# A list schedule with new planner costs: queue time apart from an instruction's end, port waits between VectorE and GpSimd, transfers by row length and with later operands

## The chip, the cores and the metric

The kernel runs on one core of one Trainium2 chip. A core has five engines that run side by side, each through a queue of its own in a fixed order: TensorE (PE, matrix products and transposes), ScalarE (ACT), VectorE (DVE), GpSimd (POOL) and SyncE (SP), which here issues all DMA transfers. An engine waits on semaphores for another engine's or a transfer's result. The metric is the time of the program on the device in microseconds (us), the median of several runs; lower is better.

## What is computed

One inference step of an encoder of two layers, for a prompt of 2048 frames and for 8 running streams of 16 new frames each, in 32-bit floating point:

```python
def prompt_layer(x, g, w_in, w_out, rel_bias, conv_w, subln_g, lam, lam_init):
    B, S, _ = x.shape
    h = rmsnorm(x, g)
    a_q, a_k, a_v, a_g, b_b, b_c, b_h, b_g, c_q, c_k, c_v, c_g = split_projection(h, w_in)
...
    o_a = band_attention_prompt(a_q.reshape(B, S, A_HEADS, HEAD_DIM), k, v, rel_bias)
...
    up = jnp.pad(b_c * b_h, ((0, 0), (CONV_WIDTH - 1, 0), (0, 0)))
    o_b = b_b * causal_conv(up, conv_w, S)
...
    o = diff_attention_prompt(cq, ck, cv, lam)
    o_c = (rmsnorm(o, subln_g, SUBLN_EPS) * (1.0 - lam_init)).reshape(B, S, C_WIDTH)
    y = x + merge_branches(o_a, a_g, o_b, b_g, o_c, c_g, w_out)
    return y, (k[:, S - keep:], v[:, S - keep:], up[:, -(CONV_WIDTH - 1):], ck, cv)
```

Branch A (8 heads) attends to the own chunk of 64 frames and 8 chunks before it, with a learned bias; B is a gated convolution of width 3; C (4 heads) takes softmax(Q1K1) - lam softmax(Q2K2) over the whole past. Each is multiplied by silu of its gate, and `w_out` brings the three back to 1024 columns.

The sample layer does the same for the running streams, over their cached keys and values. A last norm follows the second layer. Keys, values and the convolution's last rows are outputs too.

## The kernel before

The prompt is cut into 4 segments of 512 frames; a round is one segment of one layer, so there are 8 rounds. In each round a branch is a row of steps: projections (`proj_t`, `proj_n`), attention of a head (`a_attn` for A, `c_attn` for C), the convolution (`b_half`), gates, the output projection of the round before (`out_proj`) and the norm of the next one (`norm`). The small steps of the running streams (`a_sample`, `c_sample`) are put in between as tasks. Each operand of a projection is split into a high and a low part (`ah`, `al`; `whi`, `wlo`), and three matmuls take the place of one. A weight tile of 128x512 is loaded by SP (`w`, two buffers), and POOL makes `whi` and `wlo` of it (five buffers each). In an attention the scores go to PSUM (tile `s`), DVE adds the bias and takes the row's minimum (`arow` in A, `row` in C, the minimum in `sm`), ACT takes the exponential, TensorE transposes the row (tile `t`), ACT and DVE split the result into `pth` and `ptl`, and TensorE multiplies both with the values (tile `o`). In branch C q and k come back from DRAM (`cz`) through two transfers each of 64 rows of 4 KB (`q_stack`, `k_stack`). A norm takes a power of -0.5 on POOL (`rms_rows`); so does the norm of a head's output (`c_post`).

The program is not issued in the order in which it is written. Every operation is first recorded (`Program.add`), with the engine, a planned cost (`duration`), its predecessors and the buffers that it uses. `order` then plays the engines through time: of the five, that engine goes on which can start earliest, and it takes, of its instructions whose operands and buffers are there at that time by the plan, the one that was written first (projections count as written 350 places later, `LATER`). `issue` sends the instructions in that order. So the planned times have one effect, the order in each engine's queue; on the chip each queue runs in that order, and waits where the plan was wrong. `ORDER` (a list of steps for each segment) sets the order in which they are written, and is the same before and after.

Before, an instruction's end by the plan is its start plus its cost, and a user on another engine can start `LATENCY[engine][user's engine]` ns later. A transfer costs its queue 55 ns; its end is worked out from a descriptor time of 470 ns each, a start of 935 ns, 360 bytes a ns over one bus, and 850 ns.

Of the kernel before, what the change touches and what calls it, by code (L numbers as in the profile page):

```python
# [11 lines left out]
F32R = mybir.dt.float32r  # L12
BF16 = mybir.dt.bfloat16
AF = mybir.ActivationFunctionType
ALU = mybir.AluOpType
# [84 lines left out]
class Ins:  # L100
    __slots__ = ("eng", "op", "a", "k", "cost", "need", "ready", "succ", "end", "bufs", "dma", "prio", "index")


class Program:
# [5 lines left out]
    LATENCY = ((0, 198, 196, 200, 200), (270, 153, 141, 120, 140), (256, 128, 127, 155, 125), (203, 170, 65, 96, 70), (200, 110, 145, 130, 130))  # L110
# [35 lines left out]
    def duration(self, eng, op, outs, reads, k):  # L146
# [5 lines left out]
        psum = any(v.tile.tag.psum for v in big + [o for o in outs if isinstance(o, View)])  # L152
        if eng == self.PE:
            rhs = k.get("rhs")
            return 2.5 + (max(107, n / 2.4) if isinstance(rhs, View) and rhs.dt == F32R else n / 1.2)
        if eng == self.ACT:
            return (51 if psum else 93) + n / 1.2 + (186 if "accum_out" in k else 0)
        if eng == self.DVE:
            if op == "tensor_reduce":
                n = math.prod(m for _, m in big[0].v.ap[1:])  # L160
            slow = psum or len(big) > 1 or op == "tensor_reduce"
            return 70 + n / (0.96 if slow else 1.92) + (60 if len(views) > len(big) or "accum_out" in k else 0)
        return 52 + n * (2.3 if len(big) > 1 else 1.05)

    def add(self, name, op, a, k):
# [6 lines left out]
        if op == "dma_start":  # L172
            o = outs[0].v if isinstance(outs[0], View) else outs[0]
            i.cost = 55.0
            i.dma = 4.0 * math.prod(m for _, m in o.ap)
        else:
            i.cost = self.duration(i.eng, op, outs, reads, k)
        i.need, i.ready, i.succ, i.end = 0, 0.0, [], None
        i.index = len(self.ins)
# [32 lines left out]
    def order(self):  # L212
# [5 lines left out]
        dge = bus = active = 0.0  # L218
# [6 lines left out]
        def give(tag):  # L225
            while tag.head < len(tag.queue) and tag.free:
# [5 lines left out]
                for j in u.users:  # L232
                    j.need -= 1
                    j.ready = max(j.ready, t + self.LATENCY[e][j.eng])
# [11 lines left out]
        for _ in range(len(self.ins)):  # L246
# [24 lines left out]
            free[e] = t + cost  # L271
            i.end = t + cost
            if i.dma is not None:
                dge = max(dge, t + 50) + 470
                bus = max(bus, dge + 935) + i.dma / 360
                i.end = bus + 850
            out.append((t, i))
            for j in i.succ:
                j.need -= 1
                lat = self.LATENCY[e if i.dma is None else 4][j.eng]  # L280
                j.ready = max(j.ready, i.end + lat)
                if j.need == 0:
                    ready(j)
            for b in i.bufs:
                b.left -= 1
                b.end = max(b.end, (i.end, e if i.dma is None else 4))
# [1101 lines left out]
```

## Time and profile before

| | |
|---|---|
| time, median of 3 runs | 3269.55 us (3258.78 to 3273.34) |
| the profiled execution's own time | 3262.4 us |
| its span, first to last instruction | 3260.7 us |
| mean granted clock of TensorE | 0.991 |
| TensorE busy | 3055.7 us (94%), 20416 instructions |
| VectorE busy | 2326.3 us (71%) |
| ScalarE busy | 1782.0 us (55%) |
| GpSimd busy | 1648.2 us (51%) |
| share of 16 DMA engines, queue of SP | 57.1% |

The profile is of one execution. A row of instructions names the line that issues them, the engine, the operation, what is written and read by the program's names (`o<-ptl,cv`: PSUM tile `o` from `ptl` and `cv`), shape and count. All recorded operations have line 305, since `issue` sends them all; so groups are read by their tiles. A matmul's end is modelled, and matmuls overlap, so that the sum of their durations is more than the time.

### The profile page before, as it was taken

The page shows a single profiled execution, that of the slowest core. Times are in us where ns is not written, and L with a number is a line of the kernel's source. Part 1 is how long each engine was busy: PE and PEld are TensorE (multiplying, and loading weights), DVE is VectorE, ACT ScalarE, POOL GpSimd, SP SyncE. Part 2 cuts the span into 40 slices and gives each one's busy share as a digit, 9 for nine tenths or more (in the row PEclk, how much of TensorE's full clock was granted, in tenths as well). Part 3 has the DMA queues.
Part 4 walks back from the last instruction along what each step waited for, and adds up shares of the span by engine and source line. Part 5 has one row for each costly group of instructions (what it writes and reads, how often), then busy time and mean ns, then how long its engine had stood idle before and what let it go on. Part 6 is the DMA issues. An engine that isn't in the chain of part 4 may idle for free. (4 is left out here: it accounts for less than half of the span.)

```text
span 3260.7 us, 60379 instructions
## 1 busy us (share of the span) xinstructions
PE 3055.7 (94%) x20416; PEld 2764.5 (85%) x20416; DVE 2326.3 (71%) x5753; ACT 1782.0 (55%) x3817; POOL 1648.2 (51%) x1789
## 2 busy tenths in 40 slices
PE   7999899899999999999999999999899999999998
PEld 7888888788898888987888888888688988889878
DVE  3667778678685866878556576777867858587884
ACT  2654456465473654657445454665555646565652
POOL 5344564445636375453745446444555355744454
PEclk9999999999999999999999999999999999999999
DMA  6665565565655455554575655746666465655543
GB/s 209 206 183 162 162 207 169 178 191 174 199 154 167 139 186 159 161 151 128 189 220 182 179 159 182 212 150 193 213 205 189 139 185 186 190 151 159 175 119 101
DMA packets 438278, 567.51 MB, mean 174 GB/s; under 512 B 88016, under 2 KB 245200, under 8 KB 437968
## 3 DMA queue, kind: packets, MB, share of 16 engines
q1 hardware_dynamic: 437968, 563.65, 57.1%
q8 instruction: 161, 2.64, 0.3%
q14 instruction: 149, 1.22, 0.1%
HBM read 443.67 MB, written 119.84 MB: 173 GB/s over the span
## 5 line engine op out<-in xcount | busy, mean ns | idle before, releaser
L305 POOL TENSOR_SCALAR whi<-w 128x512 fp32r<-128x512 f32 x640 | 455.6, 712 | 1159.3 <-PE mm L305 705.1
L305 POOL TENSOR_TENSOR wlo<-w,whi 128x512 fp32r<-128x512 f32 x640 | 873.3, 1365 | 57.2 <-PE mm L305 8.4
L305 PE MATMUL mm<-whi,ah 128*128 128x256 f32 x2560 | 734.9, 288 | 8.3 <-ACT ah L305 5.9
L305 PE MATMUL mm<-wlo,ah 128*128 128x256 f32 x2560 | 738.0, 289 | 0.3 <-POOL wlo L305 0.2
L305 PE MATMUL mm<-whi,al 128*128 128x256 f32 x2560 | 737.2, 288 | 0.0
L305 PE MATMUL mm<-ah,whi 128*128 128x512 f32 (+2 forms) x1600 | 591.0, 370 | 7.0 <-DVE mi L305 2.3
L305 PE MATMUL mm<-al,whi 128*128 128x512 f32 (+2 forms) x1600 | 587.1, 367 | 0.0
L305 PE MATMUL mm<-ah,wlo 128*128 128x512 f32 (+2 forms) x1600 | 587.0, 368 | 0.0
L305 ACT ACTIVATE arow<-arow,sm 128x640 f32<-128x640 f32 (+4 forms) x560 | 421.1, 768 | 158.0 <-DVE sm L305 154.9
L305 PEld LDWEIGHTS mm<-whi,ah 128*128 128x128 f32 x2560 | 492.2, 193 | 15.4 <-ACT ah L305 6.2
L305 DVE TENSOR_TENSOR ptl<-t,pth 128x512 fp32r<-128x512 f32 (+3 forms) x800 | 400.7, 520 | 137.0 <-ACT pth L305 85.2
L305 PEld LDWEIGHTS mm<-wlo,ah 128*128 128x128 f32 x2560 | 492.9, 193 | 5.6 <-POOL wlo L305 0.7
L305 ACT CAST pth<-t 128x512 fp32r<-128x512 f32 (+3 forms) x800 | 346.3, 453 | 276.3 <-PE t L305 97.3
L305 PEld LDWEIGHTS mm<-whi,al 128*128 128x128 f32 x2560 | 492.9, 193 | 4.5
L305 ACT ACTIVATE row<-row,sm 128x512 f32<-128x512 f32 (+15 forms) x256 | 308.5, 1206 | 192.8 <-DVE sm L305 191.7
L305 PEld LDWEIGHTS mm<-ah,whi 128*128 128x128 f32 x1600 | 303.0, 190 | 39.6 <-POOL whi L305 2.9
L305 PEld LDWEIGHTS mm<-ah,wlo 128*128 128x128 f32 x1600 | 303.2, 190 | 28.8
L305 PEld LDWEIGHTS mm<-al,whi 128*128 128x128 f32 x1600 | 303.8, 190 | 27.9
L305 PE MATMUL t<-ident,arow 128*128 128x128 f32 x1280 | 240.7, 278 | 11.2 <-ACT arow L305 4.8
L305 PE MATMUL t<-ident,row 128*128 128x128 f32 x1360 | 214.3, 279 | 34.6 <-DVE row L305 31.3
L305 DVE SCALAR_TENSOR_TENSOR row<-row,sm,row 128x1024 f32<-128x1024 f32 (+6 forms) x115 | 199.3, 1733 | 50.8 <-POOL sm L305 44.6
L305 PE MATMUL s<-kst,qq 128*128 128x320 f32 (+4 forms) x896 | 219.8, 328 | 16.1 <-DVE sm L305 7.5
(162 smaller groups left out, 5716.6 us busy)
## 6 DMA issues: line engine op xcount, KB each, us to landing
w<-in_w_in SPq DMA_DIRECT2D x512, 256.0 KB, 3.2
w<-in_w_out SPq DMA_DIRECT2D x128, 256.0 KB, 3.1
v2a<-avh SPq DMA_DIRECT2D x112, 256.0 KB, 3.6
ch<-cz SPq DMA_DIRECT2D x96, 256.0 KB, 4.5
bias<-nbias SPq DMA_DIRECT2D x64, 320.0 KB, 3.8
avh<-qq SPq DMA_DIRECT2D x32, 512.0 KB, 3.6
q<-cz SPq DMA_DIRECT2D x64, 256.0 KB, 4.7
k<-cz SPq DMA_DIRECT2D x64, 256.0 KB, 5.9
```

Source lines behind the costliest of these rows:

```text
L305: getattr(engines[i.eng], i.op)(*[real(x) for x in i.a], **{n: real(x) for n, x in i.k.items()})
```

## The change

It edits the planner alone, in five places.

- `LATENCY` is replaced by smaller numbers, and `TAIL` is new: an engine is free for its next instruction after the cost, but the instruction ends `TAIL` later (170, 98, 83, 30 ns on PE, ACT, DVE, POOL), and users wait from that end.
- `duration` has new figures: a matmul of fp32r operands 14 + n/2.37 ns, at least 113; the power on POOL 370 + 163n; a DVE instruction with an accumulator no longer 60 ns more; others by some ns.
- Port waits: `i.port` marks DVE instructions with no PSUM operand (some kinds apart). One that starts while a POOL instruction runs by the plan is lengthened by what is left of that less 200 ns; a POOL instruction that starts while such a DVE instruction runs, by what is left less 100 ns.
- `transfer` times a DMA by the length of its contiguous runs, with 1.7 times as much for 64 partitions of long runs; its queue is busy 400 ns for each, and no more than 8 are under way.
- `LATE`: an instruction of SP counts as ready 500 ns later than its operands and buffers are.

```diff
-    LATENCY = ((0, 198, 196, 200, 200), (270, 153, 141, 120, 140), (256, 128, 127, 155, 125), (203, 170, 65, 96, 70), (200, 110, 145, 130, 130))
+    LATENCY = ((0, 36, 37, 87, 100), (53, 12, 32, 78, 60), (54, 34, 14, 83, 60), (54, 34, 34, 83, 60), (123, 23, 88, 150, 60))
+    TAIL = (170, 98, 83, 30)
+    LATE = 500
...
-            return 2.5 + (max(107, n / 2.4) if isinstance(rhs, View) and rhs.dt == F32R else n / 1.2)
+            return max(113, 14 + n / 2.37) if isinstance(rhs, View) and rhs.dt == F32R else 4 + n / 1.2
         if eng == self.ACT:
-            return (51 if psum else 93) + n / 1.2 + (186 if "accum_out" in k else 0)
+            return (51 if psum else 93) + n / 1.2 + (94 if "accum_out" in k else 0) + (94 if small else 0)
         if eng == self.DVE:
+            if op == "memset":
+                return 20 + n / 1.25
...
-            return 70 + n / (0.96 if slow else 1.92) + (60 if len(views) > len(big) or "accum_out" in k else 0)
-        return 52 + n * (2.3 if len(big) > 1 else 1.05)
+            return 70 + n / (0.96 if slow else 1.92) + (62 if small or n == 1 and len(big) > 2 else 0)
+        if op == "tensor_tensor" and k["op"] == ALU.pow:
+            return 370 + 163 * n
+        if op == "tensor_tensor":
+            return 70 + n * 2.32
+        return (80 if op == "memset" else 200 if n < 64 else 90) + n * (0.8 if op == "memset" else 1.0)
+
+    @staticmethod
+    def transfer(out, src):
+
+        runs, total = [], 4.0
+        for x in (out, src):
+            ap = x.v.ap[1:] if isinstance(x, View) else x.ap
+            run = 4
+            for st, m in reversed([d for d in ap if d[1] > 1]):
+                if 4 * st != run:
+                    break
+                run *= m
+            runs.append(min(run, 4096))
+        for _, m in (out.v if isinstance(out, View) else out).ap:
+            total *= m
+        if isinstance(out, View) and out.v.ap[0][1] == 64 and min(runs) > 2048:
+            total *= 1.7
+        return total * max(1.1 / 380, (8.5 + min(runs) / 28) / (16 * min(runs)))
...
-            i.cost = 55.0
-            i.dma = 4.0 * math.prod(m for _, m in o.ap)
+            i.cost = 400.0
+            i.dma = self.transfer(outs[0], reads[0])
...
+        i.port = i.eng == self.DVE and op not in ("memset", "reciprocal", "tensor_reduce") and not any(
+            isinstance(x, View) and x.tile.tag.psum for x in reads + outs)
...
+        gp, dv = (0.0, 0.0), (0.0, 0.0)
+        landed = []
+        late = lambda j: self.LATE if j.eng == self.SP else 0
...
-                    j.ready = max(j.ready, t + self.LATENCY[e][j.eng])
+                    j.ready = max(j.ready, t + self.LATENCY[e][j.eng] + late(j))
...
-            free[e] = t + cost
-            i.end = t + cost
             if i.dma is not None:
-                dge = max(dge, t + 50) + 470
-                bus = max(bus, dge + 935) + i.dma / 360
-                i.end = bus + 850
+                if len(landed) >= 8:
+                    t = max(t, landed[-8] + 60)
+                free[e] = t + cost
+                bus = max(bus, t + cost + 1200) + i.dma
+                i.end = max(bus + 900, t + cost + 900)
+                landed.append(i.end)
+            elif e == 0:
+                free[e] = t + cost
+                i.end = free[e] + self.TAIL[0]
+            else:
+                i.end = t + cost + self.TAIL[e]
+                if i.port and gp[0] <= t < gp[1]:
+                    i.end += max(0, gp[1] - t - 200)
+                if e == self.POOL and dv[0] <= t < dv[1]:
+                    i.end += max(0, dv[1] - t - 100)
+                free[e] = i.end - self.TAIL[e]
+                if e == self.POOL:
+                    gp = t, i.end
+                if i.port:
+                    dv = t, i.end
```

What it moves is seen at three places in the queues. In the rows, a tile's name carries the number of its buffer; the line is 305 before and 352 after.

**Place 1**, TensorE, first round: the first score matmuls of branch C (`s<-k,q`), which need q and k from DRAM; `mm` are projections. Before:

```order
L305 MATMUL mm_129<-wlo_107,ah_96 128x256
L305 MATMUL mm_129<-whi_102,al_97 128x256
L305 MATMUL mm_129<-whi_103,ah_96 128x256
L305 MATMUL s_131<-k_111,q_110 128x128
L305 MATMUL s_132<-k_111,q_110 128x128
L305 MATMUL mm_129<-wlo_108,ah_96 128x256
```

After:

```order
L352 MATMUL mm_129<-whi_104,ah_96 128x256
L352 MATMUL mm_129<-wlo_109,ah_96 128x256
L352 MATMUL mm_129<-whi_104,al_97 128x256
L352 MATMUL mm_130<-whi_102,ah_96 128x256
L352 MATMUL mm_130<-wlo_107,ah_96 128x256
L352 MATMUL s_131<-k_111,q_110 128x128
L352 MATMUL s_132<-k_111,q_110 128x128
L352 MATMUL mm_130<-whi_102,al_97 128x256
```

The same score matmul stands at place 393 of TensorE's queue before and at place 418 after, 25 later; the projections of `whi_103` and of two more weight tiles now go ahead of it.

**Place 2**, DVE and TensorE, last segment of the first layer: the splits `ptl<-t,pth` of a head of branch C and the add `mi<-mm,mi` of the output projection, which needs a part of x from DRAM. DVE before:

```order
L305 TENSOR_TENSOR ptl_127<-t_135,pth_125 128x512
L305 TENSOR_TENSOR ptl_128<-t_133,pth_126 128x512
L305 RECIPROCAL sm_85<-sm_94 128x1
L305 TENSOR_TENSOR mi_74<-mm_130,mi_74 128x512
L305 RECIPROCAL sm_92<-sm_91 128x1
L305 TENSOR_TENSOR ptl_127<-t_134,pth_125 128x512
L305 TENSOR_TENSOR ptl_128<-t_135,pth_126 128x512
```

DVE after:

```order
L352 TENSOR_TENSOR ptl_127<-t_134,pth_125 128x512
L352 TENSOR_TENSOR ptl_128<-t_135,pth_126 128x512
L352 ISA arow_68,sm_86<-s_132,bias_70,sm_86 128x320
L352 ISA sm_86 128x1
L352 TENSOR_TENSOR ptl_127<-t_133,pth_125 128x512
L352 RECIPROCAL sm_95<-sm_93 128x1
L352 TENSOR_TENSOR ptl_128<-t_134,pth_126 128x512
L352 TENSOR_TENSOR ptl_127<-t_135,pth_125 128x512
```

The same add now stands 13 instructions behind the split that it stood in front of, and a row minimum of branch A (`arow`) is between the splits. On TensorE, the two products of that split before:

```order
L305 MATMUL o_136<-pth_125,cv_117 128x256
L305 MATMUL mm_129<-whi_101,al_97 128x256
L305 MATMUL mm_129<-whi_101,ah_96 128x256
L305 MATMUL mm_129<-wlo_106,ah_96 128x256
L305 MATMUL mm_129<-whi_101,al_97 128x256
L305 MATMUL mm_129<-whi_102,ah_96 128x256
L305 MATMUL mm_129<-wlo_107,ah_96 128x256
L305 MATMUL o_136<-ptl_127,cv_117 128x256
```

And after:

```order
L352 MATMUL o_136<-pth_125,cv_117 128x256
L352 MATMUL t_135<-ident_138,row_63 128x128
L352 MATMUL t_135<-ident_138,row_64 128x128
L352 MATMUL t_135<-ident_138,row_63 128x128
L352 MATMUL s_132<-kst_120,qq_121 128x320 x2
L352 MATMUL o_136<-ptl_127,cv_117 128x256
```

Three transposes and two score matmuls of branch A stand between the two products, in place of six projections.

**Place 3**, TensorE, second segment of the second layer, a task of the running streams (`a_sample`): transposes of its row, whose splits go to `v2a`, and the products with the cached values (`o<-ch,v2a`). Before:

```order
L305 MATMUL t_133<-ident_138,arow_65 128x128 x4
L305 MATMUL t_135<-ident_138,arow_65 128x128
L305 MATMUL mm_130<-ah_98,wlo_107 128x512
L305 MATMUL mm_130<-ah_98,whi_102 128x512
L305 MATMUL mm_130<-al_99,whi_102 128x512
L305 MATMUL mm_130<-ah_98,wlo_107 128x512
L305 MATMUL mm_130<-ah_98,whi_102 128x512
L305 MATMUL mm_130<-al_99,whi_102 128x512
L305 MATMUL mm_130<-ah_98,wlo_107 128x512
L305 MATMUL o_136<-ch_113,v2a_123 128x256 x4
```

After:

```order
L352 MATMUL s_131<-ptl_128,qq_121 128x512
L352 MATMUL s_131<-pth_125,qq_121 128x512
L352 MATMUL s_132<-kst_120 128x128 x3
L352 MATMUL t_133<-ident_138,arow_65 128x128 x4
L352 MATMUL t_135<-ident_138,arow_65 128x128
L352 MATMUL s_131<-pth_126,qq_122 128x512
L352 MATMUL s_131<-ptl_127,qq_122 128x512
L352 MATMUL s_131<-pth_126,qq_122 128x512
L352 MATMUL o_136<-ch_113,v2a_123 128x256 x4
```

Three score matmuls of another task stand between, in place of seven projections, and other score matmuls of the tasks (`s<-kst`), which stood behind these products, now stand ahead of the transposes.

## Rows read from the trace of the kernel before

**Rows 1.** The page's head and its first part: busy time of each engine, share of the span, number of instructions.

```profile
span 3260.7 us, 60379 instructions
PE 3055.7 (94%) x20416; PEld 2764.5 (85%) x20416; DVE 2326.3 (71%) x5753; ACT 1782.0 (55%) x3817; POOL 1648.2 (51%) x1789
```

**Rows 2.** TensorE's waits over the whole span: its instruction's output tile, who ended the wait, then us in total, number of waits, and the longest.

```profile
PE t L305 <- DVE row L305: 31.3, 35, 9.8
PE s L305 <- DVE sm L305: 20.6, 33, 1.8
PE o L305 <- DVE ptl L305: 18.3, 26, 2.5
PE t L305 <- DVE mi L305: 11.9, 12, 3.6
PE o L305 <- DVE v2a L305: 10.7, 8, 4.6
PE s L305 <- DMA k<-cz: 8.4, 8, 1.9
PE s L305 <- POOL wlo L305: 8.0, 6, 2.2
PE s L305 <- POOL qq L305: 7.2, 8, 2.5
PE s L305 <- DVE ptl L305: 6.0, 13, 1.2
...
PE t L305 <- ACT arow L305: 4.8, 9, 1.4
PE s L305 <- DVE row L305: 4.8, 10, 0.9
PE t L305 <- POOL arow L305: 4.5, 5, 1.3
PE s L305 <- ACT pth L305: 4.0, 7, 1.7
PE s L305 <- POOL bias L305: 3.9, 3, 1.7
PE t L305 <- DVE on L305: 3.8, 4, 1.9
PE t L305 <- DVE al L305: 3.7, 3, 1.6
```

**Rows 3.** The chain that ended last, in order of time: start, us, engine and line, count. The last output projection.

```profile
3203.97 41.36 PE mm L305 x340
```

**Rows 4.** Groups of instructions, shapes apart: engine, operation, tiles, shape, count, then busy us and mean ns of one, then idle us before them. A projection matmul, a row minimum and the reading of its accumulator, the power of a norm and of a head's norm.

```profile
L305 PE MATMUL mm<-whi,ah 128*128 128x256 f32 x2560 | 734.9, 288 | 8.3 <-ACT ah L305 5.9 <-DVE gt L305 1.5 <-DVE qq L305 0.4
...
L305 DVE TENSOR_SCALAR_CACHE_REDUCE row<-s 128x512 f32<-128x512 f32 x192 | 131.4, 685 | 28.9 <-PE s L305 26.7
...
L305 DVE DVE_READ_ACCUMULATOR row<-s 128x1 f32 x192 | 15.7, 82 | 0.0
...
L305 POOL TENSOR_TENSOR sm<-sm,small 128x1 f32<-128x1 f32 x51 | 31.4, 616 | 3.4
L305 POOL TENSOR_TENSOR sm<-sm,small 128x8 f32<-128x8 f32 x16 | 28.2, 1765 | 1.2
```

**Rows 5.** The timeline from 70 to 79 us, SP's issue of q's two transfers and TensorE's first use of q and k: start us, us, engine, operation, and in brackets the idle time before it and who ended it.

```profile
70.42 2.06 SPq L305 DMA_DIRECT2D q<-cz  x2
...
78.69 0.41 PE L305 MATMUL s<-k,q 128*128 128x128 f32 x2 [1.91 <-DMA k<-cz]
```

**Rows 6.** All 64 transfers of k, from the issue to the landing.

```profile
DMA to landing us min/median/max: 4.5/5.9/9.3
```

**Rows 7.** The timeline from 2319 to 2326 us (place 3): DVE, POOL and TensorE.

```profile
2323.21 1.25 DVE L305 CAST qq<-kst 32x64 fp32r<-32x64 f32 x1
2324.80 0.49 DVE L305 TENSOR_TENSOR v2a<-bias,v2a 128x320 fp32r<-128x320 f32 x1
...
2323.15 1.26 POOL L305 TENSOR_TENSOR wlo<-w,whi 128x512 fp32r<-128x512 f32 x1
...
2325.34 1.01 PE L305 MATMUL o<-ch,v2a 128*128 128x256 f32 x3 [4.58 <-DVE v2a L305]
```

**Rows 8.** The timeline from 1279 to 1294 us (place 2): DVE, TensorE and SP, whose row is the issue of a transfer.

```profile
1292.04 0.69 DVE L305 TENSOR_TENSOR mi<-mm,mi 128x512 f32<-128x512 f32 x1 [3.48 <-DMA mi<-in_x_prompt]
1292.71 1.27 DVE L305 TENSOR_TENSOR ptl<-t,pth 128x512 fp32r<-128x512 f32 x2
...
1293.44 0.39 PE L305 MATMUL o<-ptl,cv 128*128 128x256 f32 x1 [2.55 <-DVE ptl L305]
...
1279.60 0.49 SPq L305 DMA_DIRECT2D w<-in_w_in  x1
1286.51 0.34 SPq L305 DMA_DIRECT2D w<-in_w_out  x1
...
1287.38 0.46 SPq L305 DMA_DIRECT2D mi<-in_x_prompt  x1
```

**Rows 9.** The timeline from 1588 to 1592 us, the norm of the second layer's first segment: DVE's scaling of the row and TensorE's transposes of it.

```profile
1588.89 2.30 DVE L305 SCALAR_TENSOR_TENSOR row<-row,sm,row 128x1024 f32<-128x1024 f32 x1 [0.95 <-POOL sm L305]
...
1591.24 0.98 PE L305 MATMUL t<-ident,row 128*128 128x128 f32 x7 [1.56 <-DVE row L305]
```

More of the change, by code (lines that the diff above doesn't have):

```diff
@@ L100 @@
 class Ins:
-    __slots__ = ("eng", "op", "a", "k", "cost", "need", "ready", "succ", "end", "bufs", "dma", "prio", "index")
+    __slots__ = ("eng", "op", "a", "k", "cost", "need", "ready", "succ", "end", "bufs", "dma", "prio", "index", "port")
 class Program:
@@ L152, in duration @@
         psum = any(v.tile.tag.psum for v in big + [o for o in outs if isinstance(o, View)])
+        small = len(views) > len(big)
         if eng == self.PE:
             rhs = k.get("rhs")
-            return 2.5 + (max(107, n / 2.4) if isinstance(rhs, View) and rhs.dt == F32R else n / 1.2)
+            return max(113, 14 + n / 2.37) if isinstance(rhs, View) and rhs.dt == F32R else 4 + n / 1.2
         if eng == self.ACT:
-            return (51 if psum else 93) + n / 1.2 + (186 if "accum_out" in k else 0)
+            return (51 if psum else 93) + n / 1.2 + (94 if "accum_out" in k else 0) + (94 if small else 0)
         if eng == self.DVE:
+            if op == "memset":
+                return 20 + n / 1.25
             if op == "tensor_reduce":
@@ L172, in add @@
         if op == "dma_start":
-            o = outs[0].v if isinstance(outs[0], View) else outs[0]
-            i.cost = 55.0
-            i.dma = 4.0 * math.prod(m for _, m in o.ap)
+            i.cost = 400.0
+            i.dma = self.transfer(outs[0], reads[0])
         else:
@@ L217, in order @@
         free = [0.0] * 5
-        dge = bus = active = 0.0
+        bus = active = 0.0
+        gp, dv = (0.0, 0.0), (0.0, 0.0)
+        landed = []
+        late = lambda j: self.LATE if j.eng == self.SP else 0
         window, cold = 0, True
@@ L279, in order @@
                 j.need -= 1
-                lat = self.LATENCY[e if i.dma is None else 4][j.eng]
-                j.ready = max(j.ready, i.end + lat)
+                if e or j.eng:
+                    j.ready = max(j.ready, i.end + self.LATENCY[e][j.eng] + late(j))
                 if j.need == 0:
@@ L285, in order @@
                 b.left -= 1
-                b.end = max(b.end, (i.end, e if i.dma is None else 4))
+                b.end = max(b.end, (i.end, e))
                 if b.left == 0:
```

## The prediction

> **What bounds the kernel now.** The page's first part [rows 1] comes first: TensorE (PE) is busy 3055.7 of 3260.7 us, the next engine, VectorE (DVE), 2326.3. So the time is TensorE's own work plus what it stands still for, and nothing in the change touches the work: the diff edits only the planner, and both programs hold the same 20,416 matmuls and transposes. The idle time, 3260.7 - 3055.7 = 205 us, is the first measure of what an order can save. It is too small, because a matmul's end is modelled: one 128x256 matmul shows 288 ns [rows 4], but the chain of waits ends in a stretch of 340 of them in 41.36 us [rows 3], 0.1216 us each. So each wait hides 0.288 - 0.1216 = 0.166 us more.
>
> The Trainium skill says so too (Perfetto Trace Analysis, Identifying the Most-Contended Engine): matmul busy time is a bad measure of headroom because matmuls are pipelined. Without that hidden part the sum below would come to 3232 instead of 3227.
>
> The list of TensorE's waits [rows 2] is the second view. The reader is to see that no single wait is large (the longest sum is 31.3 us) and that most name DVE or GpSimd (POOL), neither of which is full. An engine with time to spare that is late is either doing its instructions in an unlucky order or taking longer over some than the planner thought. Three stretches of the timeline then show which planned figures were wrong.
>
> **The change part by part.** It adds and removes no instruction; every cost is a place in a queue. I split the waits in two classes.
>
> **Class T: waits whose cause the old plan could not see.**
>
> *Transfers.* The first head of branch C fetches q and k by four DMAs of 64 rows. The old rule makes the fourth land at 50 + 470 + 935 + 4 x 728 + 850 = 5.2 us after the first is issued. The new one gives 400 + 1200 + 4 x 1290 + 900 = 7.7. In the trace q's first issue is at 70.42 and the matmul starts at 78.69, 8.3 us later, having waited 1.91 us [rows 5]; such a transfer takes 5.9 us to land in the median [rows 6]. The order answers: 25 more 128x256 matmuls go out before this one (place 1), 25 x 0.1216 = 3.0 us of work against a wait of 1.91. Cured, if those fillers' own weights are there; POOL, which splits them, is busy only 51% [rows 1]. TensorE's waits on k are 8.4 us in 8 [rows 2].
>
> *A load that waits, ahead of others.* SP issues all DMAs in one queue. From 1280.1 to 1286.5 us it issued nothing, because a weight load waited for its tile; a load of x behind it came out at 1287.38, a DVE add waited 3.48 us for it, and two softmax splits (`ptl`) were queued behind the add, so TensorE waited 2.55 us [rows 8]. With 0.5 us added to the time at which a transfer counts as ready, a load that waits for a tile just used falls behind those whose operands have long been there, and the add now stands behind the splits (place 2). Cured. What is late for it is the weight load: POOL, which waits for it, has its own stock of five `whi` tiles ahead of TensorE.
>
> *Powers on POOL.* The old plan takes 52 + 2.3 = 54 ns for the 128x1 power of a norm and 70 ns for 128x8; the trace has 616 and 1765 ns [rows 4], the new rule 563 and 1704. It happens 51 and 16 times. At the layer's start TensorE waits 1.56 us for the row that is scaled by it [rows 9]. TensorE's waits on such rows: `t <- DVE row` 31.3 less the 9.8 of the very first, which is the start and stays, `t <- DVE on` 3.8, `t <- DVE al` 3.7 [rows 2]: 29.0 us in 41.
>
> *DVE held by POOL.* A 32x64 cast that the plan takes for 0.19 us took 1.25, starting at 2323.21 while POOL's `wlo` ran from 2323.15 to 2324.41 [rows 7]. The new plan charges the rest of POOL's instruction less 0.2 us: 1.0 + 0.19 = 1.19. The wait there is 4.58 us. The order does not simply cure this place (place 3): the next task's score matmuls, and so the casts that feed them, now go ahead of it, which takes the casts out of its way; but only three 128x512 matmuls are left between the transposes and `o <- ch`, where seven stood. I count half. The waits of this kind: `t <- DVE mi` 11.9 and `o <- DVE v2a` 10.7, and those put down to POOL, 8.0 + 7.2 + 4.5 + 3.9 = 23.6 [rows 2]: 46.2 us in 42.
>
> Class T together: 8.4 + 29.0 + 46.2 = 83.6 us in 91 waits; with 91 x 0.166 = 15 hidden, 99 us. Bounds: nothing, if the waits only move, and all of it. I take half, -50 us, because of the places looked at two are covered fully, one in part and one is uncertain.
>
> **Class M: waits that a margin kept short.** The old plan was too slow in one thing. It let TensorE start 256 ns after DVE's planned end; the new plan 83 + 54 = 137. The trace agrees with the new one: `v2a` starts at 2324.80, takes 0.49, and TensorE starts at 2325.34 [rows 7], 0.54 us in all, where the old plan says 403 + 256 = 0.66 and the new 0.54. So 0.12 us of slack goes from every edge into TensorE, from ACT and POOL too (270 to 151, 203 to 84). A 128x256 matmul, planned at 0.1095 and now at 0.122, took 0.1216 [rows 3]; that 10% was slack as well. And one figure gets worse: a row minimum of 128x512 was 663 ns and is 603 in the new plan, plus an end of 83; the trace has 685 and then 82 ns to read the accumulator [rows 4], 0.08 us later than planned. Place 2 shows the effect: between `o <- pth` and `o <- ptl` six projection matmuls (0.73 us) stood, and now three transposes and two score matmuls, an estimate of 0.6 us. The waits of this class: 20.6 + 18.3 + 6.0 + 4.8 + 4.8 + 4.0 = 58.5 us in 98 waits [rows 2], with 16 hidden 75 us. Bounds: no growth (the engines behind run earlier as well), and doubled, +75. I take a fifth, +15: the slack lost, 0.12 us, is about a fifth of a mean wait of 0.6.
>
> **Sum.** -50 + 15 = -35 against the profiled execution of 3262.4: 3227 us. That execution lies 7 below the median of the three (3269.55) and inside their range. From the bounds: 3262 - 99 = 3163 and 3262 + 75 = 3337. Next late after the cured ones are the splits and row minima of class M, DVE's.
>
> **The rivals.**
>
> *Larger gain.* Class T goes nearly whole, and class M does not grow, since DVE and ACT run the chains earlier too: about 3262 - 95 = 3167. For it: the first k and the x load are more than covered. Against it: place 3.
>
> *Nothing moves.* Gains and losses are of one size: 3262. For it: the ends of the two classes, 99 and 75, are close, and most rows of [rows 2] are waits of about half a microsecond, which any order of this kind has.
>
> *Slower: port waits fall elsewhere than planned.* The new plan puts each collision of DVE and POOL at a certain instruction, and takes slack away at all others. If POOL runs a microsecond off the plan (its `wlo` is 1.26 us here), the collision hits another DVE instruction, and a matmul that now stands 0.12 us or more nearer waits for it. Place: the splits before `o <- ptl`. It decides from the point where class M grows by more than class T saves: with T at -20 and M doubled, 3262 - 20 + 75 = 3317. For it: DVE's cast ran to 1.25 us for reasons of timing alone. Against it: the old plan had the same collisions and no charge for them at all.
>
> The Trainium skill gives the rule behind this (SBUF — State Buffer, Who interferes with whom): the pair of ports is locked for a whole instruction, and the order of issue decides who blocks. The cast's end, 0.05 us after POOL's [rows 7], agrees. By that rule the 0.2 us that the plan takes off each wait is too kind, and a plan that is off by a fraction of a microsecond reverses who waits.
>
> **How the numbers follow.** A measurement of this kernel tells about 0.5% from no change, 16 us about 3269.55. Forecast, 3195 to 3250: 0.40. Larger gain, below 3195: 0.18. No change, 3250 to 3286: 0.21. Slower, above 3286: 0.21. So faster 0.58, same 0.21, slower 0.21. The range runs from 3155 (below the bound 3163, as small waits go too) to 3300, which leaves out about 0.05 below and 0.14 above.
>
> **What would show it.** Right: TensorE's waits on k, on `row` behind a power and on `mi` shrink to half or less; the wait at the first head of C is gone; the add near 1290 no longer holds a split up. Margins: the sum of `o <- DVE ptl`, `s <- DVE sm` and the ACT rows grows by some 10 to 20 us. Wrong if those double, if TensorE's idle time stays at 205, or if a new row heads the list, such as weights (`whi`, `wlo`) that come late because their loads are ordered 0.5 us later.

## The result and the profile after

The changed kernel takes 3281.28 us (median of 6 runs, 3278.68 to 3284.51) against 3264.11 us (6 runs, 3256.21 to 3273.34): a ratio of 1.0051, 95% interval 1.0032 to 1.0071. It is 0.5% slower; 3227 was forecast. The time lies inside the stated range (3155 to 3300), but on the other side of no change.

The head and the first part of the page after, beside [rows 1]:

```profile
span 3278.2 us, 60372 instructions
PE 3124.1 (95%) x20416; PEld 2774.5 (85%) x20416; DVE 2313.7 (71%) x5753; ACT 1778.7 (54%) x3817; POOL 1645.2 (50%) x1789
```

TensorE's idle time fell by 51 us, from 205.0 to 3278.2 - 3124.1 = 154.1. But its busy time rose by 68.4 us with the same 20,416 instructions, and that is the whole loss. TensorE's waits after, in the columns of [rows 2]:

```profile
PE t L352 <- DVE row L352: 32.2, 28, 9.0
PE s L352 <- DVE sm L352: 16.1, 21, 2.6
PE s L352 <- DVE ptl L352: 8.3, 11, 1.7
PE s L352 <- DVE row L352: 8.3, 21, 1.2
...
PE t L352 <- ACT arow L352: 5.6, 13, 0.7
PE o L352 <- DVE ptl L352: 5.4, 10, 1.2
PE t L352 <- DVE mi L352: 4.5, 12, 0.5
...
PE o L352 <- DVE v2a L352: 3.4, 6, 1.3
...
PE t L352 <- POOL arow L352: 2.2, 4, 1.3
...
PE s L352 <- ACT pth L352: 1.9, 3, 0.9
...
PE t L352 <- DVE al L352: 1.8, 2, 1.4
...
PE s L352 <- DMA k<-cz: 1.0, 2, 0.5
...
PE s L352 <- POOL bias L352: 0.3, 1, 0.3
```

Most rows that the prediction wanted to shrink shrank: `k` from 8.4 to 1.0 us, `t <- DVE mi` from 11.9 to 4.5, `v2a` from 10.7 to 3.4, and even `o <- DVE ptl` from 18.3 to 5.4; `t <- DVE row` did not. Who reads this list alone sees a faster kernel.

Where the loss sits shows in the list of the waits of TensorE's weight loads (PEld), which start ahead of their matmuls. Before:

```profile
PEld s L305 <- DVE sm L305: 38.6, 63, 2.0
PEld o L305 <- DVE ptl L305: 32.9, 53, 2.8
...
PEld s L305 <- DVE row L305: 15.1, 36, 1.4
...
PEld t L305 <- ACT arow L305: 11.2, 21, 1.6
```

After:

```profile
PEld s L352 <- DVE sm L352: 52.7, 136, 3.1
...
PEld s L352 <- DVE row L352: 35.6, 95, 1.6
PEld o L352 <- DVE ptl L352: 23.2, 76, 1.5
...
PEld t L352 <- ACT arow L352: 14.8, 37, 1.1
```

These are waits for row minima and splits; their number doubles, and each is short. Over the whole list there are 426 before and 653 after, with a sum of 314.9 and 311.4 us. One of the short ones, in the timeline of the changed kernel (ScalarE's split, then TensorE):

```profile
452.26 0.37 ACT L352 CAST pth<-t 128x256 fp32r<-128x256 f32 x1
...
452.41 0.28 PE L352 MATMUL mm<-whi,ah 128*128 128x256 f32 x1
...
452.68 0.19 PEld L352 LDWEIGHTS o<-pth,cv 128*128 128x128 f32 x1 [0.20 <-ACT pth L352]
452.68 0.39 PE L352 MATMUL o<-pth,cv 128*128 128x256 f32 x1
```

The split ends at 452.63 and the product starts at 452.68, 0.27 us after the matmul ahead of it; the matmuls around it start 0.12 apart. So TensorE stood for 0.15 us. But the matmul ahead has a modelled end at 452.69, so the PE row has no bracket: the stand counts as busy.

**A count that sees them.** From the trace I took the time between the starts of two matmuls that follow each other, less what a pair of these output tiles and shapes takes when nothing is late (the 15th percentile of such pairs over both traces; 2772 us in all before, 2774 after), less the time lost at the lower clock. What is left in steps of 20 to 200 ns I call *short stands*, above that *long* ones. Before: 176 us in 2289 short ones, 240 in long ones, 23 lost at the low clock. After: 239 us in 3125, 194, 22. The change took 46 us out of the long stands and put 63 into short ones. (The expectations of e1 to e4 were written with an earlier form of this count, which gave 194 us of short stands before and 256 after.)

The places of the prediction after, each found again as the same instruction. In the timeline's order: place 1 [rows 5], place 2 [rows 8] (the split's product, and the add), the norm [rows 9] and place 3 [rows 7]:

```profile
80.08 0.41 PE L352 MATMUL s<-k,q 128*128 128x128 f32 x2 [0.52 <-DMA k<-cz]
...
1285.97 0.28 PE L352 MATMUL o<-ptl,cv 128*128 128x256 f32 x1
...
1296.61 0.69 DVE L352 TENSOR_TENSOR mi<-mm,mi 128x512 f32<-128x512 f32 x1 [2.46 <-PE mm L352]
...
1597.75 0.72 POOL L352 TENSOR_SCALAR bias<-bias 128x640 f32<-128x640 f32 x1 [0.56 <-DMA bias<-in_rel_b]
...
1599.52 0.57 POOL L352 TENSOR_TENSOR sm<-sm,small 128x1 f32<-128x1 f32 x1
...
1600.12 2.27 DVE L352 SCALAR_TENSOR_TENSOR row<-row,sm,row 128x1024 f32<-128x1024 f32 x1 [0.97 <-POOL sm L352]
...
1602.45 0.90 PE L352 MATMUL t<-ident,row 128*128 128x128 f32 x3 [3.36 <-DVE row L352]
...
2324.86 0.79 PE L352 MATMUL s<-pth,qq 128*128 128x512 f32 x1 [0.93 <-ACT pth L352]
...
2326.55 1.57 DVE L352 TENSOR_TENSOR v2a<-bias,v2a 128x320 fp32r<-128x320 f32 x1
...
2326.68 0.80 PE L352 MATMUL s<-ptl,qq 128*128 128x512 f32 x1 [1.02 <-DVE ptl L352]
...
2328.17 1.22 PE L352 MATMUL o<-ch,v2a 128*128 128x256 f32 x4 [0.27 <-DVE v2a L352]
```

TensorE's wait for k went from 1.91 to 0.52 us, the split's from 2.55 to nothing, the one for `v2a` from 4.58 to 0.27, though the score matmuls that now stand ahead of it waited 0.93 and 1.02 us themselves. The norm's grew from 1.56 to 3.36: its power ran behind work of POOL that waited for a load.

### The profile page after: what moved, and what is told of

Same layout as the page of the kernel before. It is cut to its first block, busy times and chain, and to the rows that moved or that the text cites. A ratio compares the mean times of both kernels' runs of the same rounds, so it can differ in the third digit from the quotient of the medians.

```text
span 3278.2 us, 60372 instructions
## 1 busy us (share of the span) xinstructions
PE 3124.1 (95%) x20416; PEld 2774.5 (85%) x20416; DVE 2313.7 (71%) x5753; ACT 1778.7 (54%) x3817; POOL 1645.2 (50%) x1789
## 5 line engine op out<-in xcount | busy, mean ns | idle before, releaser
L352 PE MATMUL s<-kst,qq 128*128 128x320 f32 (+4 forms) x896 | 226.7, 338 | 8.6 <-DVE sm L352 5.0
L352 DVE SCALAR_TENSOR_TENSOR row<-row,sm,row 128x1024 f32<-128x1024 f32 (+6 forms) x115 | 208.1, 1810 | 27.7 <-POOL sm L352 25.9
```

Source lines behind the costliest of these rows:

```text
L352: getattr(engines[i.eng], i.op)(*[real(x) for x in i.a], **{n: real(x) for n, x in i.k.items()})
```

## The experiments

Each time is a median; each ratio is to runs of the kernel before on the same chip, with its 95% interval. The last three columns are of the profiled execution, counted as above (us); "low clock" is the time lost there, not the time spent there.

| kernel | time | ratio | short | long | low clock |
|---|---|---|---|---|---|
| before | 3264.11 | 1 | 176 | 240 | 23 |
| after | 3281.28 | 1.0051 (1.0032 to 1.0071) | 239 | 194 | 22 |
| e2_control1 | 3274.66 | 1.0054 (1.0035 to 1.0072) | 236 | 194 | 24 |
| e9_part_T | 3240.16 | 0.9934 (0.9920 to 0.9947) | 160 | 212 | 39 |
| e10_part_M | 3425.01 | 1.0492 (1.0471 to 1.0512) | 258 | 319 | 26 |
| e3_latency_only | 3269.00 | 1.0041 (1.0024 to 1.0058) | 191 | 233 | 19 |
| e15_others_only | 3271.72 | 1.0037 (1.0023 to 1.0051) | 175 | 243 | 21 |
| e13_matmul_only | 3392.75 | 1.0413 (1.0398 to 1.0429) | 222 | 317 | 33 |
| e4_dma_pow_only | 3292.67 | 1.0118 (1.0097 to 1.0140) | 174 | 260 | 32 |
| e5_no_port | 3355.91 | 1.0282 (1.0263 to 1.0301) | 253 | 254 | 19 |
| e6_old_dma | 3304.90 | 1.0125 (1.0106 to 1.0144) | 242 | 209 | 24 |
| e12_full_port | 3303.43 | 1.0124 (1.0109 to 1.0138) | 223 | 220 | 37 |
| e14_old_matmul | 3236.91 | 0.9931 (0.9914 to 0.9947) | 172 | 208 | 34 |
| e1_margin120 | 3250.73 | 0.9976 (0.9963 to 0.9990) | 201 | 202 | 23 |
| e8_margin240 | 3252.24 | 0.9966 (0.9948 to 0.9984) | 182 | 213 | 39 |
| e7_accum82 | 3274.12 | 1.0034 (1.0022 to 1.0047) | 202 | 216 | 32 |
| e11_margin_accum | 3221.84 | 0.9878 (0.9865 to 0.9891) | 179 | 193 | 24 |
| e16_margin_accum_oldmm | 3276.27 | 1.0053 (1.0038 to 1.0068) | 150 | 246 | 56 |
| e17_middle | 3245.67 | 0.9950 (0.9935 to 0.9965) | 161 | 215 | 42 |
| e18_before_more | 3264.33 | 1.0015 (1.0002 to 1.0027) | 167 | 244 | 29 |

### A first look: slack, chance, parts

Theory (margin): the long waits went as forecast, but the plan lost its slack. Rivals: the charges for collisions do harm (port), or any new order scatters by as much (chance).

**e1_margin120**, on the changed kernel:

```diff
-    LATENCY = ((0, 36, 37, 87, 100), (53, 12, 32, 78, 60), (54, 34, 14, 83, 60), (54, 34, 34, 83, 60), (123, 23, 88, 150, 60))
+    LATENCY = ((0, 36, 37, 87, 100), (173, 12, 32, 78, 60), (174, 34, 14, 83, 60), (174, 34, 34, 83, 60), (123, 23, 88, 150, 60))
```

> The changed kernel with one thing given back: a user on TensorE counts as able to start 120 ns later after ACT, DVE and POOL, which is the slack of the old plan. Margin theory (the long waits went as forecast, but operands now arrive just when the plan has them, and matmuls that stand still for 20 to 200 ns each took the gain back): these short stands, 256 us after against 194 before, fall by 40 to 60 us, the long waits stay short, and the time is 3220 to 3245 us. Port theory (the loss comes from the charges for collisions of DVE and POOL, which fall elsewhere on the chip): unchanged, 3272 to 3290. Chance theory (any other order of this kind scatters by some 20 us): anywhere from 3255 to 3290, with no relation to the short stands.

0.75% less than the changed kernel (1.0051 to 0.9976). Short stands fell by 38 us and long ones rose by 8. The margin theory has the direction; the time is some 6 us above its range. It is below the ranges of the two rivals.

**e2_control1**: the same edit with 54, 55 and 55 in place of 173, 174 and 174.

> The changed kernel with 1 ns instead of 120 in the same three places: a control that tells how far a change of order without meaning moves the time. Margin and port theory: within 0.25% of the changed kernel, 3273 to 3289 us. Chance theory: off by 10 us or more, either way.

The ratio is that of the changed kernel within 0.03%, though 18% of TensorE's instructions stand at another place (2.3 places off in the mean over all). So a small shuffle doesn't move the time. It doesn't settle how far orders scatter that differ more: in e1 72% stand elsewhere (8.9 places), and between before and after 80% (14.4 places).

**e3_latency_only**, on the kernel before (between two instructions of TensorE the plan then waits no longer, as in the change):

```diff
-    LATENCY = ((0, 198, 196, 200, 200), (270, 153, 141, 120, 140), (256, 128, 127, 155, 125), (203, 170, 65, 96, 70), (200, 110, 145, 130, 130))
+    LATENCY = ((0, 36, 37, 87, 100), (53, 12, 32, 78, 60), (54, 34, 14, 83, 60), (54, 34, 34, 83, 60), (123, 23, 88, 150, 60))
+    TAIL = (170, 98, 83, 30, 0)
...
-            i.end = t + cost
+            i.end = t + cost + self.TAIL[e]
...
```

> The kernel before with only the new LATENCY and TAIL; costs, transfers, port waits as before. Margin theory: the slack is lost and no long wait is cured, so 40 to 60 us slower than before, 3300 to 3325 us. Port theory: no port charges in it, so as before, 3255 to 3272. Chance theory: within 20 us of before, either sign.

Only 10 us slower, and 15 us more of short stands. The margin theory in the form "latencies" fell: they cost far less than expected, and the time lies where the port and the chance theory had it. If slack was the cause, most of what was lost had to be elsewhere.

**e4_dma_pow_only**, on the kernel before, with all of the change's rules for transfers and its cost of a power:

```diff
...
-            i.cost = 55.0
-            i.dma = 4.0 * math.prod(m for _, m in o.ap)
+            i.cost = 400.0
+            i.dma = self.transfer(outs[0], reads[0])
...
+        late = lambda j: 500 if j.eng == self.SP else 0
...
```

> The kernel before with only the new rules for transfers (by row length, 400 ns of queue, 8 under way, 500 ns later operands) and the new cost of a power on POOL; slack as before and no port charges. Margin theory: the gain of the cured waits without the loss, 30 to 50 us less than before, 3215 to 3235 us, TensorE's long waits (over 0.5 us) down from 203 to 150 to 175 us and the short stands unchanged at about 194. Port theory: also faster, by 20 to 50. Chance theory: within 20 us of before.

All theories missed: 34 us slower, 20 more in long stands and 9 more at the low clock. Transfers and powers planned nearer to how they run don't help by themselves. Why they hurt in this order stays open.

### Undoing one part in the changed kernel

**e5_no_port**:

```diff
-                if i.port and gp[0] <= t < gp[1]:
-                    i.end += max(0, gp[1] - t - 200)
-                if e == self.POOL and dv[0] <= t < dv[1]:
-                    i.end += max(0, dv[1] - t - 100)
```

> The changed kernel without the charges for collisions of DVE and POOL; all else as changed. If these charges are what shortened the long waits (those over 0.2 us, 194 us after against 240 before), they come back to 220 to 240 us and the time is 3295 to 3315 us. If the charges are what brought the short stands (20 to 200 ns, 239 us after against 176 before), these fall to about 200 us and the time is 3240 to 3260. If neither, within 8 us of the changed kernel.

Without the charges the changed kernel loses another 2.3% of 3263, 75 us, more than any case had. Long stands go from 194 to 254. Among TensorE's waits the one for the additions on `mi` is back, above [rows 2] even:

```profile
PE t L348 <- DVE mi L348: 16.9, 22, 2.7
```

**e6_old_dma**: the old transfer lines back, 55 ns of queue, `LATE = 0`.

```diff
-    LATE = 500
+    LATE = 0
...
-                bus = max(bus, t + cost + 1200) + i.dma
-                i.end = max(bus + 900, t + cost + 900)
+                dge = max(dge, t + 50) + 470
+                bus = max(bus, dge + 935) + i.dma / 360
+                i.end = bus + 850
```

> The changed kernel with the old rules for transfers (55 ns of queue, 470 + 935 ns, 360 bytes a ns, 850 ns, no later operands); all else as changed. Theory that the new transfer rules lose (they alone, with the powers, made the kernel before 1.2% slower, with long waits 260 instead of 240 us and 109 instead of 62 us at the low clock): long waits fall by 10 to 25 us, time 3240 to 3262 us. Theory of the prediction (transfers planned as they run save waits): k is late again and loads hold others up, 3290 to 3310 us.

24 us slower (1.0125 against 1.0051). The prediction's theory holds here: the waits on transfers are back.

```profile
PE s L351 <- DMA k<-cz: 12.2, 9, 3.5
...
PE s L351 <- DMA q<-cz: 9.9, 6, 2.2
PE s L351 <- DMA ch<-cz: 7.8, 4, 4.2
```

Together with the cost of a power these rules lost 34 us on the old plan, and they gain 24 here (the power's cost stays): a part's worth depends on what the others leave.

**e7_accum82**:

```diff
-            return 70 + n / (0.96 if slow else 1.92) + (62 if small or n == 1 and len(big) > 2 else 0)
+            return 70 + n / (0.96 if slow else 1.92) + (62 if small or n == 1 and len(big) > 2 else 0) + (82 if "accum_out" in k else 0)
```

> The changed kernel with 82 ns more for each DVE instruction that has an accumulator (row minima), as the trace has it for reading the accumulator. If undercosted row minima are a main source of the short stands: these fall by 15 to 30 us and the time to 3250 to 3268 us. If the slack into TensorE as a whole is the source and not this figure: short stands within 10 us of 239, time 3270 to 3288.

Short stands fell by 37 us, more than expected, but long ones rose by 22 and the low clock took 10 more; the time fell by only 0.17%, which is within the intervals.

**e8_margin240**: the edit of e1 with 293, 294 and 294.

> The changed kernel with 240 ns more into TensorE after ACT, DVE and POOL, twice the slack given back before. If slack goes on paying: short stands from 201 us (at 120 ns) towards 176, time 3225 to 3245 us. If 120 ns was about the best and what is added now only moves work about: short stands 185 to 205, long waits up by 10 to 20, time 3248 to 3268.

No better than 120 beyond the intervals: 19 us less in short stands, 11 more in long ones, 16 more at the low clock.

### The two halves of the prediction, each alone

**e9_part_T** is e4 with the charges for collisions added (the four lines of e5, put into the kernel before).

> The kernel before with the half of the change that plans what the old plan could not see: transfers, powers and the charges for collisions of DVE and POOL; LATENCY and all other costs as before (class T of the prediction alone). By the prediction it saves some 50 us: 3205 to 3225 us. Theory now (the old, slower latencies had covered the collisions already; charges on top of them buy little, and the transfers without the charges cost 34 us): 3255 to 3285 us.

20.5 us faster, so the prediction has the sign and is more than twice too high: 28 us less in long stands and 16 in short ones, with 16 more at the low clock. With e4 it says that on the old plan too the charges are worth 34 + 20.5 = 54 us. My theory that they would buy little there fell.

**e10_part_M** is the changed kernel with the edits of e5 and e6 and the old cost of a power.

> The other half: the new LATENCY, TAIL and costs of instructions, with the old transfers, the old power and no charges for collisions (class M of the prediction alone). By the prediction it costs 15 us, at most 75: 3275 to 3335 us. Theory now (slack was what covered collisions and late transfers; without it each of them costs, and in the changed kernel the charges were worth some 75 us and the transfers 24): about before + 20 + 75 + 24, 3360 to 3400 us.

164 us slower, more than any sum I had: 82 us more in short stands, 79 in long ones.

### Which figure of class M

**e13_matmul_only**, on the kernel before:

```diff
-            return 2.5 + (max(107, n / 2.4) if isinstance(rhs, View) and rhs.dt == F32R else n / 1.2)
+            return max(113, 14 + n / 2.37) if isinstance(rhs, View) and rhs.dt == F32R else 4 + n / 1.2
```

> The kernel before with the new cost of a matmul only (128x256 at 0.122 us in place of 0.1095). The half M cost 164 us, and the new latencies alone 11. If the matmul's cost is the main slack (planned 10% too fast, it put 10% more matmuls under each wait than the plan thought it needed): 60 to 120 us slower than before, 3320 to 3380 us. If the other costs are: within 15 us of before. If M costs only as a whole, since each slack stands in for the others: 10 to 40 us slower, 3270 to 3300.

One line costs 134 us: 46 in short stands, 77 in long ones, 10 at the low clock, which makes 133. Its page and some of its waits:

```profile
span 3395.8 us, 60430 instructions
PE 3132.4 (92%) x20416; PEld 2775.2 (82%) x20416; DVE 2327.9 (69%) x5753; ACT 1786.7 (53%) x3817; POOL 1626.3 (48%) x1789
```

```profile
PE t L305 <- DVE row L305: 44.0, 46, 8.9
...
PE s L305 <- DMA k<-cz: 16.6, 8, 4.1
...
PE s L305 <- ACT pth L305: 12.4, 15, 2.1
PE s L305 <- DVE ptl L305: 12.4, 21, 2.4
...
PE t L305 <- ACT arow L305: 10.2, 15, 2.9
```

Waits of many kinds are up, those for transfers among them (k: 8.4 to 16.6), which no latency of an engine touches.

**e15_others_only**: the new lines for ACT, DVE and POOL in `duration`, the power apart, on the kernel before.

```diff
-            return (51 if psum else 93) + n / 1.2 + (186 if "accum_out" in k else 0)
+            return (51 if psum else 93) + n / 1.2 + (94 if "accum_out" in k else 0) + (94 if small else 0)
...
-            return 70 + n / (0.96 if slow else 1.92) + (60 if len(views) > len(big) or "accum_out" in k else 0)
+            return 70 + n / (0.96 if slow else 1.92) + (62 if small or n == 1 and len(big) > 2 else 0)
```

> The kernel before with only the new costs of instructions on ACT, DVE and POOL (accumulators among them; the power as before). If these make the most of M's 164 us: 60 to 120 us slower than before, 3320 to 3380. If the matmul's cost does: within 20 us of before, 3245 to 3285. If M costs only as a whole: 10 to 40 us slower.

13 us slower, 0.4%. So the three parts of class M, each alone, make 10 + 13 + 134 = 157 of its 164 us.

**e14_old_matmul**: the edit of e13 the other way, on the changed kernel.

> The changed kernel with the old cost of a matmul. If the 10% are the main slack: 30 to 60 us less than the changed kernel, 3220 to 3250 us, short stands from 239 to 190 or less. If other costs are: within 10 us of it, 3270 to 3290.

1.2% less than the changed kernel, faster than before, and short stands at 172. The number of weight loads' waits for row minima is near that of before again (72 and 62, where 136 and 95 stood):

```profile
PEld s L352 <- DVE sm L352: 41.0, 72, 8.9
PEld s L352 <- DVE row L352: 26.5, 62, 1.2
PEld o L352 <- DVE ptl L352: 15.5, 41, 1.3
```

### How much slack

**e11_margin_accum**: e1 and e7 together.

> The changed kernel with both repairs, 120 ns of slack into TensorE and 82 ns for an accumulator. If they mend different short stands: short stands about 170 to 180 us, time 3235 to 3250 us, the lowest so far. If they mend the same ones, as the first is a remedy for the second: 3248 to 3262, no better than the slack alone (3251).

3222 us, 1.2% less than before and the lowest of all: short stands as before, long ones as after. The time is below both cases, and the two together give more (1.7%) than the sum of each alone (0.75 + 0.17%), so they hardly mend the same stands.

```profile
PEld s L352 <- DVE sm L352: 31.1, 63, 1.8
PEld o L352 <- DVE ptl L352: 16.4, 44, 1.1
PEld s L352 <- DVE row L352: 15.7, 41, 0.9
```

**e16_margin_accum_oldmm**: e11 with the edit of e14.

> The changed kernel with all three repairs: 120 ns into TensorE, 82 ns for an accumulator (these two gave 3222 us) and the old cost of a matmul. If slack still lacks: 3195 to 3215 us. If the two were enough: 3215 to 3235, with the low clock and the long waits making the difference.

54 us worse than e11, and outside both cases. Short stands are the lowest (150), but long ones are up by 53 us and the low clock takes 32 more. Too much slack is one reading and not shown: e9, with the old slack and class T, took 3240.

**e17_middle**: 60 ns in place of 120, and the new cost of a matmul times 0.95.

```diff
-            return max(113, 14 + n / 2.37) if isinstance(rhs, View) and rhs.dt == F32R else 4 + n / 1.2
+            return 0.95 * max(113, 14 + n / 2.37) if isinstance(rhs, View) and rhs.dt == F32R else 4 + n / 1.2
```

> The changed kernel with slack between the two best: 60 ns into TensorE, 82 ns for an accumulator and a matmul planned 5% too fast (120 and 82 ns gave 3222 us, the same with a matmul 10% too fast 3276). If the time is a smooth curve of the slack with its lowest point about there: 3212 to 3230 us. If it jumps by some 20 us from order to order: 3230 to 3260.

Not a smooth curve: short stands lie between, as they should, but long ones and the low clock are above e11's.

**e18_before_more**: 0.95 times the cost of a matmul in the kernel before.

> The kernel before with a matmul planned 5% faster still (15% faster than it runs). With the matmul's cost right the kernel before lost 134 us. If it still lacks slack: 3225 to 3252 us, with less time in long waits (240 us). If 10% was about enough: 3255 to 3290 us, with more time at the low clock.

Within 0.3% of before, in the second case: more slack of this kind did not help the kernel before.

**e12_full_port**, on the changed kernel:

```diff
-                    i.end += max(0, gp[1] - t - 200)
+                    i.end += max(0, gp[1] - t)
...
-                    i.end += max(0, dv[1] - t - 100)
+                    i.end += max(0, dv[1] - t)
```

> The changed kernel with the charges for collisions in full: without the 200 and 100 ns that the plan takes off. If the plan's charges are too kind, long waits and short stands both fall, by 10 to 25 us in all: 3255 to 3272 us. If the charges hit other instructions than the plan has, larger ones misplace more: 3285 to 3310 us. If 0.1 to 0.2 us at some hundreds of places doesn't matter: 3274 to 3288 us.

0.7% slower than the changed kernel, with fewer short stands (223) but more long ones and 15 us more at the low clock. The charges as they stand are the better ones.

## Why the prediction was wrong

**The step that failed is class M, "+15, a fifth".** Its half of the change alone costs 164 us (e10), above its upper bound of 75; within the change it shows as 63 us more of short stands, four times the forecast. The prediction did see that the planned matmul went from 0.1095 to 0.122 us and called the 10% slack, but gave them no price: it priced the class by the 0.12 us of the latencies, which alone cost 10 us (e3). The matmul's cost alone costs 134 (e13) and, put back, returns some 40 (e14). The reason is argued, and fits the queues: 0.12 us is taken once from an edge, while 10% is taken from all the work that covers it. Between the last score matmul of a row of branch A and the first transpose that needs the row (288 rows, start to start, each matmul at its unhindered time) TensorE has, in the first quartile, 4.25 us of work before, 4.23 with the new latencies alone, 3.68 with the matmul's cost alone, 4.00 after and 4.46 with the old matmul's cost in the changed kernel. The plan also keeps an account of TensorE's clock, into which the matmul's cost goes, and plans matmuls twice as long where it holds the clock to be low. But it has 27 us of such stretches before and 20 in e13, too little to be behind 134 us. In the trace a 128x256 matmul starts 0.120 us after the one ahead (median of 10,943). So the old figure was wrong, and by this reading its error was a reserve of some 9% under every chain.

**The base of that term was too small as well.** It scaled the 58.5 us of waits that the list shows. After the change these rows are down to 45.6 us in 79, while 63 us came as short stands that the list doesn't hold, since up to 0.166 us of each hides behind a modelled end. The prediction used that figure to make visible waits dearer, and not to ask how many others it hides. Its sign for the margins misled likewise: `o <- DVE ptl`, `s <- DVE sm` and the ACT rows were to grow by 10 to 20 us and fell from 47.7 to 29.0. The page of the Trainium skill that it cited (Perfetto Trace Analysis, Identifying the Most-Contended Engine) names the weight loads' busy share, beside the share of peak operations, instead of matmul time. Here that busy share is 85% before and after, so it doesn't show the loss either. The number of the weight loads' waits does, between these two kernels.

**Class T was right within the change in its sum, but not by itself.** Its waits went from 83.6 to 36.4 us: k 8.4 to 1.0, `mi` and `v2a` 22.6 to 7.9, the four of POOL 23.6 to 2.5. That is 47, where half of 83.6 was forecast; TensorE's idle time in neither class grew by 10 us meanwhile, 53.1 to 63.1 (the idle time less the two classes and the start's wait of 9.8 and 9.0). "Half" is an average of rows that went nearly whole and rows that hardly moved, so that the sum fits is in part luck. The part on powers was wrong: `row` (less the start's 9.0) and `al` make 25.0 where 29.0 stood, and the norm looked at got worse. Alone, class T is worth 20.5 us (e9). On top of class M it is worth 144 (3425 to 3281); that without slack each collision and each late transfer counts is the likely reason, not a tried one. So the two classes can't be summed: -20.5 + 164 would be 3408.

**The rivals.** *Nothing moves* (3250 to 3286, given 0.21) holds the measured time, and its reason, gains and losses of one size, is what the stands show: 46 us against 63. *Larger gain* needed a class M that does not grow. The slower one had the condition right (class M grows by more than class T saves) and the cause wrong. It held the charges for collisions responsible; they are the best part of the change (e5: 75 us, e9 against e4: 54).

The rule that it drew from the Trainium skill (SBUF — State Buffer, Who interferes with whom), that the 0.2 us taken off are too kind, is borne out by a little. The `v2a` subtraction above ran 1.57 us, beside a `wlo` of POOL from 2326.01 to 2327.76. The plan's rule, 0.40 + 0.08 + (2327.76 - 2326.55 - 0.2), gives 1.49, and the full charge 1.69. Over the whole traces, DVE instructions without a PSUM operand (memsets, reciprocals and accumulator reads apart) that started while a POOL instruction had more than 0.3 us left were longer by what was left less 0.14 us (median of 298 before and of 277 after), and those with a PSUM operand were no longer at all (749 and 769). So 0.2 is some 0.06 too much, and no deduction is 0.14 too little; that e12 is slower speaks of its order, not against the rule.

**The signs to look for.** "Wrong if TensorE's idle time stays at 205" was a bad sign: it fell to 154 and the kernel got slower.

Open stay why the rules for transfers and powers alone lose 34 us (e4), and how much of the differences among e1, e8, e11, e16 and e17 is slack and how much the luck of one order.

## What to carry to other kernels

In a list schedule a cost that is wrong in the safe direction is slack; before it is put right, its share of the work under each chain is to be priced, and the slack put back on purpose where the trace shows operands arriving last (here 120 ns into TensorE and 82 ns for an accumulator turned +0.5% into -1.2%). Where matmul ends are modelled, a change is to be judged by the time from start to start, not by idle time. The number of weight-load waits helps (426 before, 653 after) but doesn't suffice: e16 has the fewest, 361, and takes 3276 us. Parts of a planner are to be tried alone and taken out one by one, as here the matmul's cost was worth 134 us alone and some 40 in the changed kernel.

## What the runs showed of the hardware

The orders differ in the time that TensorE spends at 1.2 instead of 2.4 GHz, which I had not expected. Slack alone doesn't order them: by the count above the low clock took 23 us before, 23 in e1 and 24 in e11, which have more slack than the changed kernel (22), but 39 in e8 and 56 in e16, which have more still, and 33 in e13, which has less than the kernel before. The mean granted clock was 0.991 before, 0.988 in e11, 0.982 in e14, and in e16:

```profile
core 0: 3277.4 us, clock 0.969
```

Three stretches of 16.4 us there, one behind the other, the columns being the stretch, its length, TensorE's busy time and count, the granted clock, the DMA share and GB/s:

```profile
2279.60:2296.00 16.40, 16.08 (x82) 1.00 1.04 325
2296.00:2312.40 16.40, 8.16 (x41) 0.85 0.72 243
2312.40:2328.80 16.40, 10.67 (x31) 0.52 0.43 133
```

TensorE was busy for 16.08 us at the full clock, then for only 8.16 us, in which the clock fell (0.85 in the mean), and then for 10.67 us, with 31 matmuls, at nearly the lower clock throughout. So here the fall followed a stretch in which TensorE stood for half of the time. Whether that holds for the other falls, and what in an order brings such stretches about, was not tried apart.

The trace also gives a price for DVE and POOL in each other's way: what is left of POOL's instruction less 0.14 us, and nothing where DVE reads or writes PSUM (the counts stand with the rivals).
